# The output projection of a hybrid attention layer, summed in groups of two and four chunks in place of groups of two

## The chip, the cores and the metric

The kernel runs on one core of one Trainium2 chip. The metric is device time in microseconds (us) of one execution, lower is better; the kernel before stands at 1275.82 us, the median of three runs (1275.24 to 1278.71). Engines go by the names of the profile: PE is the matrix engine (PEld its weight loads), DVE the vector engine, ACT the scalar engine, POOL the general engine, SP the engine that issues the DMAs. A line such as L728 is line 728 of the kernel before.

## The reference, cut to what matters

One layer of width 1024 over 1024 tokens and 16 meta tokens. Three mixers read the same normalised input, their outputs are concatenated to 1024 columns and go through one projection, whose result is added to the residual; a gated feed-forward network follows.

```python
a = rmsnorm(h, norm1[i])
proj = a @ w_in[i]
...
y_pool = multiscale_pool_mixer(u, pool_w[i], pool_scale[i])
y_fox = head_rmsnorm(forgetting_attention(...), fox_out_gain[i], FOX_HEADS)
y_sb = head_rmsnorm(stick_breaking_attention(...), sb_out_gain[i], SB_HEADS)
h = h + jnp.concatenate([y_pool, y_fox, y_sb], axis=-1) @ w_out[i]
a = rmsnorm(h, norm2[i])
h = h + (jax.nn.silu(a @ w_gate[i]) * (a @ w_up[i])) @ w_down[i]
```

## The kernel before

Every fp32 product is made of three matmuls on split operands: each operand is split into a high part and the rest (tiles whose names end in h and l), and high times high, high times low and low times high are summed in PSUM.

The concatenated mixer output has eight chunks of 128 columns: 0 and 1 come from the pooling mixer, 2 to 4 from the forgetting heads, 5 to 7 from the stick-breaking heads. The six head pairs are worked one after another (`PAIRS`, L70), in the order of chunks 5, 2, 3, 4, 6, 7. Each finished chunk but the last is stored to HBM (`ysd`, L588); the last pair's result is kept on chip (`last_y`, L595).

The output projection (L690 to L763) takes the chunks in the groups `OGROUPS = ((5, 2), (3, 4), (0, 1), (6, 7))` (L782) and the tokens in two halves of 512 (j = 1, then j = 0). For a group and a half, `out_load` (L733) loads and splits what it needs: the group's weights once, by `split_weights` (L690), and the chunks' activations, by `split_y` (L711). Each 128x512 piece comes by a DMA on SP and is split by two instructions on POOL: a TENSOR_SCALAR for the high part (L77) and a TENSOR_TENSOR for the rest (L708 for weights, L717 for activations). `out_part` (L738) then calls `out_block` (L720) for each of four blocks of 128 tokens, and that for each 512 columns sums the group in one PSUM tile (six matmuls for two chunks, L728) and adds the tile into the residual `h` on DVE (L730). There are four groups, two halves, four blocks and two column halves, so 64 additions. The PSUM tiles have two buffers (tag `mm`). Of the split tiles there are few: group 0 and group 2 share four weight tiles `xa` of the pool `x0`, group 1 and group 3 share four tiles `wa`, and the split activations have eight tiles `xb`, two to a chunk, so eight tiles hold two parts of two chunks.

All this runs beside the attention of the last pairs. `interleave` (L815) takes steps of two streams in turn: `attention()` (L572) at a higher priority, and `filler()` (L857), which yields the projections of later pairs and then, from `open_out` (L840) on, the parts of the output projection in the order (0, 1), (0, 0), (1, 1), (1, 0), (2, 1), (2, 0) of group and half. The last group follows in `out_last` (L745), half 1 beside the attention's tail (L886), half 0 behind it (L933); for each block it also makes the norm of the finished rows on ACT (L753 to L760), and `turn_block` (L765) transposes them on PE (L771) for the feed-forward part. The framework then orders the instructions of each engine by its own forecast and the priorities, so the order on an engine is not that of the source. Each engine works its own list strictly in order.

The attention's own steps in these stretches: scores on PE (L465, L467, mask L470), ACT functions (L497 to L503), a scan on DVE (L506) and a subtraction (L508), an exponential (L510), transposes on PE (L560), their split by ACT (L563) and DVE (L564), and the weighted sum on PE (L549); at the end of a head pair's half a norm (L424 to L451, with a POOL split to `pt` and the matmuls L430, L431).

Behind it stands the feed-forward part: two column chunks are made directly (`direct`, L953), while DVE and ACT make sums and splits of the normalised rows (L974 to L981); then come ten rounds of a Strassen scheme (`strassen`, L992), whose products are matmuls of L917 on operands `t` and `s`, with weights that are combined on POOL (L1016, L999) and split by ACT (L903) and DVE (L905). The first combination needs a load of `w_gate` (L910) into space that the operands of those sums leave.

## Time and profile before

| what | value |
|---|---|
| median of three runs | 1275.82 us |
| the profiled execution's own time | 1275.61 us |
| its span, first to last instruction | 1273.8 us |
| outside the span | 1.8 us |
| mean granted PE clock | 0.986 |
| PE busy | 1214.1 us, 95% of the span |
| DVE busy | 904.7 us, 71% |
| ACT busy | 625.1 us, 49% |
| POOL busy | 469.2 us, 37% |

Output projection work on PE begins at 461.6 us of the span and ends at 626 us; the first Strassen product that needs a combined weight starts at 671.7 us. The page gives busy time, instructions and waits of each engine; "idle before" and what stands in square brackets is how long the engine waited for the instruction and which instruction released it. Matmuls overlap, so the pace of a stream of them is read from one start to the next and not from the duration of one.

### The profile page before, as it was taken

The numbers are of one execution on the slowest core, as the hardware profiler recorded it, in microseconds if no ns is written. First come the engines' busy times: TensorE is split into PE (matmuls) and PEld (weight loads), VectorE is DVE, ScalarE is ACT, GpSimd is POOL, SyncE is SP. The second block draws the span as 40 slices with busy tenths as digits, with TensorE's granted clock in tenths as the row PEclk, the third lists the DMA queues.
The fourth block names the chain that finished last, engine by engine and source line by source line (L and its number), as shares of the span: only waits on it lengthen the run. The fifth ranks groups of instructions, "written<-read, shape, count | busy, mean of one in ns | idle before, by whom it ended". The sixth has DMA issues, their size and how long they took to land.

```text
span 1273.8 us, 18454 instructions
## 1 busy us (share of the span) xinstructions
PE 1214.1 (95%) x6370; PEld 1027.3 (81%) x6370; DVE 904.7 (71%) x1573; ACT 625.1 (49%) x1283; POOL 469.2 (37%) x537
## 2 busy tenths in 40 slices
PE   7898899999898989998999999999999999999997
PEld 6787788899887877787787888888888888788885
DVE  6768866667857679997687667666676656866557
ACT  6567655455547676778644233333233334444443
POOL 3376154553366774440105444434444401000001
PEclk9899899999999989999999999999999999999999
DMA  8001010010110161101514545434555449576653
GB/s 327 30 17 35 10 59 19 30 38 26 42 34 25 47 240 51 58 25 67 191 57 142 190 165 159 155 127 156 190 172 167 134 137 334 173 223 195 194 174 140
DMA packets 74330, 151.38 MB, mean 119 GB/s; under 512 B 9197, under 2 KB 21485, under 8 KB 74237
## 3 DMA queue, kind: packets, MB, share of 16 engines
q1 hardware_dynamic: 70912, 146.27, 34.5%
q10 hardware_dynamic: 3324, 3.95, 0.9%
q8 instruction: 50, 0.82, 0.3%
q14 instruction: 44, 0.35, 0.1%
HBM read 108.24 MB, written 41.94 MB: 118 GB/s over the span
## 4 chain that ended last, share of the span: by engine, by line
PE 70%; DVE 14%; issue 6%; ACT 4%; DMA 4%; POOL 1%; SPq 0%; DVEq 0%; POOLq 0%; ACTq 0%
PE s L917 22%; PE mm L299 12%; PE mm L917 8%; PE s L1102 7%; PE mm L728 4%; DVE r L506 4%; PE o L549 4%; PE s L560 3%; PE mm L1102 3%; PE o L1102 3%; PE s L465 2%; PE s L467 1%; DVE P L508 1%; DMA wr<-in_w_in 1%; DVE pl L564 1%
## 5 line engine op out<-in xcount | busy, mean ns | idle before, releaser
L917 PE MATMUL s<-t,wh 128*128 128x512 f32 x544 | 170.2, 392 | 2.5 <-ACT wh L903 2.5
L917 PEld LDWEIGHTS s<-t,wh 128*128 128x128 f32 x544 | 102.8, 189 | 24.4 <-ACT wh L903 3.1
L917 PE MATMUL s<-s,wh 128*128 128x512 f32 x384 | 119.4, 391 | 0.3 <-ACT wh L903 0.3
L564 DVE TENSOR_TENSOR pl<-s,ph 128x512 fp32r<-128x512 f32 (+1 forms) x168 | 91.8, 568 | 32.4 <-ACT ph L563 28.5
L903 ACT CAST wh<-ss 128x512 fp32r<-128x512 f32 x80 | 49.5, 621 | 132.1 <-PE s L917 98.4
L563 ACT CAST ph<-s 128x512 fp32r<-128x512 f32 (+1 forms) x168 | 78.8, 493 | 67.0 <-PE o L549 38.3
L917 PE MATMUL s<-t,wl 128*128 128x512 f32 x272 | 106.1, 391 | 0.0
L917 PE MATMUL mm<-t,wh 128*128 128x512 f32 x320 | 98.7, 389 | 0.0
L1090 ACT CAST wh<-sg 128x512 fp32r<-128x512 f32 x74 | 46.0, 623 | 106.9 <-PE o L1102 45.2
L299 PE MATMUL mm<-x,wh 128*128 128x512 f32 (+1 forms) x320 | 97.8, 379 | 0.4 <-DVE pt L364 0.4
L903 ACT CAST wh<-raw 128x512 fp32r<-128x512 f32 x68 | 41.7, 620 | 108.4 <-PE s L917 69.9
L1091 DVE TENSOR_TENSOR wl<-sg,wh 128x512 fp32r<-128x512 f32 x74 | 50.9, 689 | 58.4 <-ACT wh L1090 58.1
L560 PE MATMUL s<-identr,P 128*128 128x128 f32 x528 | 82.6, 280 | 9.3 <-DVE P L508 4.1
L917 PEld LDWEIGHTS s<-s,wh 128*128 128x128 f32 x384 | 71.7, 188 | 15.8 <-ACT wh L903 1.1
L1011 DVE TENSOR_TENSOR cg<-s,tmp 128x512 f32<-128x512 f32 x60 | 41.3, 688 | 59.5 <-PE s L917 59.5
L549 PE MATMUL o<-pl,v 128*128 128x256 f32 (+1 forms) x288 | 82.5, 310 | 0.6 <-DVE pl L564 0.6
L299 PE MATMUL mm<-xa,wh 128*128 128x264 f32 (+3 forms) x248 | 77.5, 314 | 4.2 <-DVE v L358 3.8
L1141 POOL TENSOR_TENSOR r<-r,mhalf 128x1 f32<-128x1 f32 x8 | 4.4, 548 | 208.4 <-DVE r L1140 206.9
L560 PEld LDWEIGHTS s<-identr,P 128*128 128x128 f32 x528 | 63.6, 143 | 18.7 <-DVE pl L564 3.4
L549 PE MATMUL o<-ph,v 128*128 128x256 f32 (+1 forms) x288 | 77.6, 284 | 0.0
L299 PE MATMUL mm<-xb,wh 128*128 128x264 f32 (+3 forms) x248 | 76.9, 311 | 0.0
L299 PE MATMUL mm<-xa,wl 128*128 128x264 f32 (+3 forms) x248 | 76.5, 312 | 0.0
(290 smaller groups left out, 3548.2 us busy)
## 6 DMA issues: line engine op xcount, KB each, us to landing
sg<-lsd SPq DMA_DIRECT2D x70, 256.0 KB, 2.9
raw<-in_w_gate SPq DMA_DIRECT2D x22, 512.0 KB, 5.3
raw<-in_w_up SPq DMA_DIRECT2D x22, 512.0 KB, 4.0
wr<-in_w_in SPq DMA_DIRECT2D x80, 128.0 KB, 2.3
raw<-in_w_down SPq DMA_DIRECT2D x20, 512.0 KB, 3.5
lsd<-cg SPq DMA_DIRECT2D x40, 256.0 KB, 3.4
raw<-rsd SPq DMA_DIRECT2D x40, 256.0 KB, 3.4
raw<-in_w_down SPq DMA_DIRECT2D x34, 256.0 KB, 3.0
```

Of the source, the lines that this page charges most:

```text
L299: PE.matmul(p[:, :n], w[k][ww], xx(k, t0, n), start=i == 0, stop=i == 23)
L506: V.tensor_tensor_scan(r[:, ::-1], e[:, ::-1], (e if on_dve else r)[:, ::-1], 0.0 if prev is None else prev[:, 0:1], ALU.add, ALU.max if o ...
L549: PE.matmul(po[:, c:256], pr.v[h][:, kb, :], x, start=first and ix == 0, stop=(kb == nkb - 1 and ix == 1), skip_group_check=True)
L560: PE.transpose(tp[:, 128 * i:128 * i + 128], ptiles[ii][:, k0:k0 + 128], ident)
L563: S.copy(ph[:, :n], tp[:, :n])
L564: V.tensor_tensor(pl[:, :n], tp[:, :n], ph[:, :n], ALU.subtract)
L728: PE.matmul(p, y_[:, ts_], w_[:, ds], start=i == 0, stop=i == 3 * len(ws) - 1)
L903: S.copy(wh, a)
L917: PE.matmul(p, ws[ww][:, k, :], xs_[xx][:, k, :], start=first and i == 0, stop=i == 11, skip_group_check=True)
L1090: S.copy(wh, a)
L1091: V.tensor_tensor(wl, a, wh, ALU.subtract)
L1102: PE.matmul(p, x[xx][:, 128 * b:128 * b + 128], y[yy], start=first and i == 0, stop=last and i == 2, skip_group_check=True)
```

## The change

Groups can now be summed together: `out_load` and `out_part` take a tuple of groups. The order becomes group 0 for half 1, groups 0 and 1 together for half 0, groups 1 and 2 together for half 1, group 2 for half 0, and the last group for both halves as before. A joint part sums twelve matmuls in one PSUM tile and makes one addition for it, so 64 additions become 48. The matmuls, the loads and the splits are the same in number; a joint part holds all eight `xb` tiles at once. The lines below `out_load` move by up to three (L771 becomes L773, L917 becomes L920).

```diff
-    def out_load(g, j):
-        if g not in wts:
-            wts[g] = [split_weights(g, c) for c in OGROUPS[g]]
-        return [last_y[j] if c == PAIRS[5][3] else split_y(c, j) for c in OGROUPS[g]]
+    def out_load(gs, j):
+        for g in gs:
+            if g not in wts:
+                wts[g] = [split_weights(g, c) for c in OGROUPS[g]]
+        return [last_y[j] if c == PAIRS[5][3] else split_y(c, j) for g in gs for c in OGROUPS[g]]
...
-    def out_part(g, j, yy=None):
+    def out_part(gs, j, yy=None):
         if yy is None:
-            yy = out_load(g, j)
+            yy = out_load(gs, j)
         for tb in range(4):
-            yield from out_block(4 * j + tb, tb, yy, wts[g])
+            yield from out_block(4 * j + tb, tb, yy, [w for g in gs for w in wts[g]])
...
-        for g, j in ((0, 0), (1, 1), (1, 0), (2, 1), (2, 0)):
-            yield from out_part(g, j)
+        yield from out_part((0, 1), 0)
+        yield from out_part((1, 2), 1)
+        yield from out_part((2,), 0)
```

The first place is POOL's list where group 2's weights are split for the first time (`xa` from `wor`), with the activations of the next part (`xb` from `yr`); `pt` belongs to the attention's norm. Before, the weights (`xa`, `wor`) take turns with the activations of another part, group 1's half 0 (`xb_6995` to `xb_7003`):

```order
L77 TENSOR_SCALAR xa_7219<-wor_7221 128x512
L77 TENSOR_SCALAR xb_6995<-yr_6993 128x512
L77 TENSOR_SCALAR xa_7219<-wor_7225 128x512
L708 TENSOR_TENSOR xa_7220<-wor_7221,xa_7219 128x512
L717 TENSOR_TENSOR xb_6997<-yr_6993,xb_6995 128x512
L77 TENSOR_SCALAR xb_7001<-yr_6999 128x512
L708 TENSOR_TENSOR xa_7220<-wor_7225,xa_7219 128x512
L717 TENSOR_TENSOR xb_7003<-yr_6999,xb_7001 128x512
L77 TENSOR_SCALAR xa_7229<-wor_7231 128x512
```

In the changed kernel the same place on POOL, from the norm's split `pt` to the first part of chunk 0's activations (`xb_7011`), whose rest `xb_7013` comes three rows later and whose partner chunk 1 is split by the two rows after that:

```order
L717 TENSOR_TENSOR xb_7001<-yr_6997,xb_6999 128x512
L77 TENSOR_SCALAR xb_7005<-yr_7003 128x512
L77 TENSOR_SCALAR pt_6793<-nt_6791 128x512
L77 TENSOR_SCALAR xa_6987<-wor_6989 128x512
L717 TENSOR_TENSOR xb_7007<-yr_7003,xb_7005 128x512
L77 TENSOR_SCALAR xa_6987<-wor_6993 128x512
L77 TENSOR_SCALAR xb_7011<-yr_7009 128x512
L708 TENSOR_TENSOR xa_6988<-wor_6989,xa_6987 128x512
L708 TENSOR_TENSOR xa_6988<-wor_6993,xa_6987 128x512
L717 TENSOR_TENSOR xb_7013<-yr_7009,xb_7011 128x512
```

Eight weight splits, eight activation splits and one split of the norm now stand in one run behind one wait for PE, all of them ahead of the last matmuls of the first joint tile of groups 1 and 2; before, the weights of group 2 were split while group 1's own part had its operands already.

The second place is PE's list at the transposes of the last normalised block (L771 on `xa`), among the matmuls of the direct products; `s_8272` is the third of those products, `s_8299` the fourth. Before:

```order
L917 MATMUL s_8272<-s_7948,wl_8042 128x512
L771 MATMUL o_8180<-identr,xa_8136 128x128 x4
L917 MATMUL s_8299<-s_7945,wh_8046 128x512
L917 MATMUL s_8299<-s_7946,wh_8046 128x512
L917 MATMUL s_8299<-s_7945,wl_8048 128x512
L917 MATMUL s_8299<-s_7945,wh_8046 128x512
L771 MATMUL o_8186<-identr,xa_8136 128x128 x4
L917 MATMUL s_8299<-s_7946,wh_8046 128x512
```

In the changed kernel the third product is `s_8240`:

```order
L920 MATMUL s_8240<-s_7913,wl_8006 128x512
L920 MATMUL s_8240<-s_7913,wh_8004 128x512
L773 MATMUL o_8148<-identr,xa_8104 128x128 x4
L773 MATMUL o_8154<-identr,xa_8104 128x128 x4
L920 MATMUL s_8240<-s_7914,wh_8004 128x512
L920 MATMUL s_8240<-s_7913,wl_8006 128x512
```

The last transposes now stand in the third direct product and not in the fourth: from them to the first matmul that needs a combined weight there are 148 matmuls of that line in the list, where there were 128.

## The prediction

> **What bounds the kernel now.** I read the busy times first, then the stretches around the output projection, then who PE waited for there, and last the rows of each wait. The busy times say that PE is the bound:

> ```profile
> PE 1214.1 (95%) x6370; PEld 1027.3 (81%) x6370; DVE 904.7 (71%) x1573; ACT 625.1 (49%) x1283; POOL 469.2 (37%) x537
> ```

> The matmuls stay the same in number, so the change can only win or lose idle time of PE. The table of stretches (length, then busy time of PE, PEld, DVE, ACT and POOL, the granted clock, DMA) says where that is:

> ```profile
> 481.23:502.43 21.20, 19.49 (x109) 16.05 (x107) 18.30 (x32) 15.27 (x37) 6.47 (x7) 1.00 0.08 26
> 502.43:522.40 19.97, 17.21 (x79) 13.27 (x80) 19.03 (x29) 12.25 (x26) 15.68 (x15) 1.00 0.31 97
> ...
> 553.00:575.00 22.00, 21.60 (x121) 17.78 (x120) 21.36 (x37) 15.10 (x36) 4.47 (x4) 1.00 0.00 1
> 575.00:601.00 26.00, 23.00 (x147) 19.82 (x147) 19.33 (x41) 22.48 (x54) 1.24 (x2) 1.00 0.15 61
> 601.00:616.00 15.00, 11.68 (x53) 7.95 (x52) 14.88 (x25) 12.91 (x25) 1.09 (x2) 1.00 0.51 176
> ...
> 668.00:677.00 9.00, 6.53 (x22) 4.80 (x21) 5.37 (x5) 4.53 (x8) 7.21 (x6) 0.81 0.21 75
> 677.00:1273.80 596.80, 587.13 (x2589) 485.63 (x2587) 400.11 (x561) 207.41 (x357) 164.02 (x113) 1.00 0.54 177
> ```

> PE is idle for 1.7 and 2.8 us in the two stretches from 481 to 522, where groups 0 and 1 are summed, for 3.0 and 3.3 us at the end of the attention, and for 2.5 us near 670. Behind 677 it is idle for 9.7 us of 597, and the order there is the same in both kernels, so that part only shifts. From 502 to 522 DVE is busy for 19.03 of 19.97 us: there DVE is the rival of PE. The waits of PE, from 461 to 680 us (total, times, longest):

> ```profile
> PE mm L728 <- DVE x L730: 5.5, 7, 1.6
> ...
> PE s L917 <- ACT wh L903: 2.7, 2, 2.5
> PE s L560 <- DVE P L508: 2.2, 2, 1.8
> PE s L771 <- ACT xa L760: 1.7, 1, 1.7
> ```

> **Term A, the additions that go.** One addition takes 681 ns (minimum, median, maximum in the row), and 16 of them, 10.9 us of DVE, go:

> ```profile
> L730 DVE TENSOR_TENSOR x<-mm,x x64: 657/681/692, 465.2 to 626.2; 128x512 f32<-128x512 f32 x64
> ```

> DVE's time is not PE's. What PE feels is that a PSUM tile comes free late, when an addition stands behind the attention's scans. Four of the seven waits lie where tiles are now joined (the number in brackets is the wait):

> ```profile
> 502.43 1.66 PE L728 MATMUL mm<-wa,xb 128*128 128x512 f32 x6 [1.48 <-DVE x L730]
> ...
> 504.95 1.66 PE L728 MATMUL mm<-wa,xb 128*128 128x512 f32 x6 [0.20 <-DVE x L730]
> ...
> 507.70 1.67 PE L728 MATMUL mm<-wa,xb 128*128 128x512 f32 x6 [0.97 <-DVE x L730]
> ...
> 522.40 1.67 PE L728 MATMUL mm<-wa,xb 128*128 128x512 f32 x6 [1.57 <-DVE x L730]
> ```

> They sum to 4.2 us. A joint tile gives the addition twice the time, twelve matmuls and not six, 2.8 us and not 1.4 by the starts in the next rows; the longest wait, 1.57, is about what is added. I take A = -4.2; the bounds are 0 (other DVE work takes the place) and -5.5 (all seven).

> **Term B, the loads that can't run ahead.** The pace of PE's work, from starts: 12 matmuls in 2.82 us, 0.235 each; score matmuls 0.16 to 0.2; transposes 0.11, weighted sums 0.12:

> ```profile
> 513.97 0.32 PE L465 MATMUL s<-k,q 128*128 128x348 f32 x1
> 514.12 0.32 PE L467 MATMUL s<-k,q 128*128 128x348 f32 x1
> 514.28 2.97 PE L728 MATMUL mm<-wa,xb 128*128 128x512 f32 x12
> 517.10 0.32 PE L465 MATMUL s<-k,q 128*128 128x348 f32 x1
> ```

> ```profile
> 538.28 0.88 PE s L560 x8
> ...
> 542.48 0.48 PE o L549 x4
> ```

> And of POOL's splits (the last row of a run is its end; the brackets are waits):

> ```profile
> 480.19 0.62 POOL L77 TENSOR_SCALAR xb<-yr 128x512 fp32r<-128x512 f32 x1 [2.37 <-PE mm L728]
> 480.90 1.28 POOL L717 TENSOR_TENSOR xb<-yr,xb 128x512 fp32r<-128x512 f32 x1
> ...
> 499.80 1.28 POOL L77 TENSOR_SCALAR xa<-wor 128x512 fp32r<-128x512 f32 x1 [6.40 <-PE mm L728]
> ...
> 512.50 1.30 POOL L708 TENSOR_TENSOR xa<-wor,xa 128x512 fp32r<-128x512 f32 x1
> ...
> 537.43 0.63 POOL L77 TENSOR_SCALAR wa<-wor 128x512 fp32r<-128x512 f32 x1 [13.87 <-PE mm L728]
> ...
> 541.20 2.03 POOL L717 TENSOR_TENSOR xb<-yr,xb 128x512 fp32r<-128x512 f32 x1
> ...
> 545.04 1.31 POOL L717 TENSOR_TENSOR xb<-yr,xb 128x512 fp32r<-128x512 f32 x1
> ```

> At 499.80 POOL begins with group 2's weights as soon as group 0's last tile has read its own; the run of 12 splits ends at 513.80, 1.17 us each. PE did not wait for it, since group 1's part had its operands. In the changed kernel nothing lies between: the joint part of groups 1 and 2 needs all eight `xb` tiles, and the joint part ahead of it holds them to its last tile. Counted in the order, from the third matmul of that last tile (which frees the first `xa`) PE has 25 matmuls of the projection, 8 of scores, 2 of the norm, 17 transposes and 11 weighted sums ahead of the first matmul on the rest of chunk 0: 25 x 0.235 + 8 x 0.17 + 2 x 0.235 + 17 x 0.11 + 11 x 0.12 = 10.9 us. By then POOL has to make 15 splits (7 of the rest, 8 of the high part). At 0.62 and 1.28 they take 13.9 us, at 1.17 each 17.6. So PE halts for 3.0 to 6.7 us. The halt is in pieces, as each operand comes, and all that stands behind these matmuls in PE's list, the attention's transposes too, halts with it. DVE is less loaded here than at 499.80 but not idle, so I take 1.09 each, 16.4, and a halt of 5.5, nearer to the measured run of 12 than to the free pace. The DMAs of these pieces are issued ahead, except the last three, which wait for a buffer of POOL's and land within the run; SP has nothing else queued there.

> The next part, group 2 alone, has the same: the same eight splits as at 537.43, where chunk 0 was ready 5.8 us behind the release (541.20 + 2.03) and chunk 1 8.9 us (545.04 + 1.31). By the same paces PE has 5.0 and 8.1 us of work until it needs them, so 0.8 us more. At the first boundary there is none: chunk 3 and 4 of half 0 wait for PE as at 480.19, and their four splits are ready 4.4 us later, when PE is still in the first two chunks. B = +6.3, bounds 3.0 and 7.5.

> [...]

> **Term C, the end.** PE's list has the third direct product's matmuls behind the last transposes, 148 matmuls to the Strassen product with the first combined weight, where there were 128. In the profile:

> ```profile
> 639.53 0.60 PE L771 MATMUL o<-identr,xa 128*128 128x128 f32 x4
> ...
> 668.79 0.39 PE L917 MATMUL mm<-t,wl 128*128 128x512 f32 x1
> 671.66 1.74 PE L917 MATMUL s<-t,wh 128*128 128x512 f32 x4 [2.47 <-ACT wh L903]
> ...
> 675.88 0.39 PE L917 MATMUL s<-t,wh 128*128 128x512 f32 x1
> ```

> The chain from those transposes over DVE's sums, the load of `w_gate` (whose space they free), POOL and ACT takes 671.66 - 639.53 = 32.1 us. 128 matmuls take 29.1 (639.88 to 669.0, 0.228 each), 148 take 33.7; so PE would arrive 1.9 us behind the weight and not 2.5 ahead of it. The wait also costs pace: the 11 matmuls from 671.66 to 675.88 take 4.2 us for 2.5, since the clock was halved:

> ```profile
> 673.00:675.00 2.00, 2.00 (x6) 1.52 (x6) 2.00 (x3) 0.88 (x2) 1.52 (x1) 0.50 0.00 0
> ```

> ```profile
> 580.84 0.83 PE L560 MATMUL s<-identr,P 128*128 128x128 f32 x5 [1.84 <-DVE P L508]
> ```

> C = -(2.5 + 1.7) = -4.2, bounds 0 and -4.2. Next in line are the following weights, which stand ready behind 672 while PE takes 2.8 us for each product. A wait of 1.84 (above, 1.00 in its stretch) did not halve the clock and one of 2.47 did. Of B's pieces none is over 2.3 by the count; one over 2.5 would cost 1.7 more. [...]

> **Term D, the tail.** In 575 to 616 PE waits for the attention's last latency and for the norm of the blocks. The order puts two half tiles of the last group behind the attention's last weighted sums, where before they filled them: 6 matmuls, 1.4 us, if nothing else covers, 0 if they fill a later wait. D = +0.7. The rest of the 6.3 us idle there I leave as it is.

> **Sum.** The profiled execution took 1275.61 us, a span of 1273.8 and 1.8 around it, 0.2 below the median of the three. 1275.6 - 4.2 + 6.3 - 4.2 + 0.7 = 1274.2.

> **Rivals.** First, faster: POOL's run goes at its free pace, since DVE halts with PE and leaves it alone; B = 3.0 and D = 0, 1275.6 - 4.2 + 3.0 - 4.2 = 1270.2, and 1269 with all of A's bound. For it: splits of 0.62 and 1.28 stand in the rows; against: runs of a dozen never kept that pace.

> Second, slower: the halt is paid twice. In DVE's list the additions of the first two joint tiles of groups 1 and 2 stand ahead of the attention's next subtraction and scan, so DVE halts for POOL's run too, and its backlog moves into the stretch that was 553 to 575, where DVE was busy for 21.36 of 22.00 us; PE then waits there for the tiles as it did at 502, and A is 0. With B at 7.5, D at 1.4 and C as above: 1275.6 + 7.5 + 1.4 - 4.2 = 1280.3. It decides from a POOL run over 17.6 us (1.17 a split). Against it: DVE has 10.9 us less to do.

> Third, the change at the far end does not come: the chain to the first combined weight moves along with PE, and the 2.5 us and the slow clock stay: 1275.6 - 4.2 + 6.3 + 0.7 = 1278.4.

> **How the numbers follow.** A measurement of this kernel can tell about 0.3%, 3.8 us, from no change: faster is below 1272.0, slower above 1279.6. The forecast has 0.45 (its own range 1272 to 1277 by B's bounds), the first rival 0.30, the second 0.13, the third 0.12. Faster is most of the first rival and the forecast's lower end, 0.34; slower is the second and the third's upper end, 0.15; the rest, 0.51, is no change. The range goes from the first rival with A's bound, 1269, to the second, 1280.5.

> **What would show it.** Right: 48 additions, no wait of L728 for L730 over 0.5 us in the joint parts; waits of L728 for POOL's splits of 4 to 7 us in total, at the start of the joint part of groups 1 and 2; no wait of the first combined product, full clock there. The forecast is wrong if PE does not wait for POOL (then it is nearer 1270), or if waits for DVE's additions or scans come back behind that part, or if the wait near 670 is still there.

## The result, and the profile after

The changed kernel took 1282.21 us (median of 7 runs, 1280.84 to 1284.34), the kernel before 1278.08 beside it: a ratio of 1.0039, interval 1.0027 to 1.0051. A second set gave 1281.44 to 1277.76, 1.0022 (1.0010 to 1.0034). So the change makes the kernel slower by 0.2 to 0.4%, about 4 us. Both intervals lie above 1. The forecast was 1274.2, range 1269.0 to 1280.5, 1.4 us faster than its profiled execution: the sign was wrong, and the time lies above the range.

The profiled execution has a span of 1282.6 us, 8.8 longer than before, and not all of that is the change's: it is the slowest of its seven executions (1284.34 us), and that of the second profile the slowest of its eight (1283.94), while the forecast's profile of before (1275.61) lies near the fast end of the seven executions of before (1275.24 to 1278.71). The first page shows it: PE has the same 6370 matmuls, is busy for 6.9 us more and idle for 1.9 more, at a mean granted clock of 0.978 in place of 0.986.

```profile
PE 1221.0 (95%) x6370; PEld 1033.4 (81%) x6370; DVE 899.4 (70%) x1557; ACT 625.0 (49%) x1283; POOL 470.4 (37%) x537
```

Since both run 6370 matmuls, the start of the n-th can be laid beside the start of the n-th before. The difference grows or shrinks only where one of them loses time (us, against the first profile of before; "again" are second profiles of the same kernels):

| stretch of matmuls (times before) | before again | changed | changed again | forecast |
|---|---|---|---|---|
| 0 to 2340 (7 to 391), same list | +1.6 | +1.3 | +0.9 | |
| to 2470 (413), same list | +2.2 | +2.4 | +2.4 | |
| to 2860 (485), same list | +0.5 | -1.2 | -1.4 | |
| to 2990 (512) | 0.0 | -2.7 | -2.7 | A |
| to 3120 (539) | 0.0 | +7.6 | +7.7 | A's last wait, B |
| to 3640 (640) | +1.2 | +2.8 | +2.9 | B's second part, D |
| to 3870 (697) | -1.6 | -4.4 | -4.4 | C |
| to 5590 (1087), same list | 0.0 | 0.0 | 0.0 | |
| to 5720 (1118), same list | +0.9 | +3.0 | +3.0 | |

In the four rows where the lists differ, the changed kernel loses 3.2 and 3.4 us, where the forecast had a gain of 1.4. The rows above them are the same instructions in both kernels, and differ by as much between two profiles of one kernel. The waits of PE there, of the changed kernel from 511 to 535 us (engine and matmul, what it waited for, total, times, longest):

```profile
PE s L560 <- DVE P L508: 3.0, 2, 1.9
PE s L465 <- DVE P L508: 0.7, 1, 0.7
PE s L560 <- DVE pl L564: 0.7, 1, 0.7
PE mm L728 <- POOL xb L717: 0.6, 1, 0.6
PE o L431 <- DVE nt L428: 0.3, 1, 0.3
```

They add up to 5.3 us, nearly the 5.5 of the forecast halt, but 0.6 of it is for POOL's late pieces and 4.7 for DVE, whose part the forecast had at nothing. The table of stretches (length, busy PE, PEld, DVE, ACT, POOL, granted clock) says what more was lost:

```profile
505.00:513.10 8.10, 8.10 (x40) 6.56 (x39) 8.00 (x15) 3.90 (x9) 0.00 (x0) 1.00 0.09 34
513.10:526.60 13.50, 9.93 (x46) 6.71 (x45) 9.97 (x13) 10.35 (x23) 13.47 (x13) 1.00 0.25 78
526.60:536.80 10.20, 8.45 (x32) 6.95 (x31) 7.52 (x10) 5.35 (x11) 6.02 (x5) 0.50 0.41 129
536.80:561.00 24.20, 24.20 (x137) 20.57 (x137) 17.78 (x29) 14.43 (x34) 0.00 (x0) 1.00 0.00 1
561.00:580.00 19.00, 15.66 (x80) 12.09 (x79) 17.07 (x26) 13.07 (x33) 18.28 (x16) 1.00 0.14 43
```

From 505 to 513.1 PE is never idle: the waits of 502 to 508 us are gone, as forecast. Then POOL works its 17 splits without a break (POOL busy 13.47 of 13.50), PE idles for 3.6 us, and the clock stands at half for 10.2 us. A second run of POOL, 16 splits from 561, costs PE 3.3 us more, all of it waits for the additions, which stand behind the scans in DVE's list:

```profile
566.29 1.22 PE L728 MATMUL mm<-xa,xb 128*128 128x512 f32 x4 [0.43 <-DVE x L730]
...
571.89 3.05 PE L728 MATMUL mm<-xa,xb 128*128 128x512 f32 x12 [1.28 <-DVE x L730]
...
578.90 1.65 PE L728 MATMUL mm<-xa,xb 128*128 128x512 f32 x6 [1.61 <-DVE x L730]
```

Between the runs, with POOL idle, PE loses nothing.

What POOL's run does to DVE is seen in the groups of DVE's instructions by shape (busy time, mean ns of one), both in the changed kernel. From 497 to 513 us, where POOL is idle:

```profile
L508 DVE TENSOR_TENSOR P<-s,r 128x456 f32<-128x456 f32 x2 | 1.2, 614 | 0.0
...
L506 DVE TENSOR_TENSOR_SCAN r<-e 128x456 f32<-128x456 f32 x1 | 1.1, 1108 | 0.0
...
L506 DVE TENSOR_TENSOR_SCAN r<-e,r 128x348 f32<-128x348 f32 x1 | 0.9, 942 | 0.0
...
L451 DVE SCALAR_TENSOR_TENSOR nt<-op,gn,nt 128x512 f32<-128x512 f32 x1 | 0.7, 741 | 0.0
```

From 513 to 533 us, beside POOL's run:

```profile
L506 DVE TENSOR_TENSOR_SCAN r<-e,r 128x456 f32<-128x456 f32 x2 | 3.8, 1910 | 2.3 <-ACT e L503 2.3
...
L451 DVE SCALAR_TENSOR_TENSOR nt<-op,gn,nt 128x512 f32<-128x512 f32 x1 | 1.7, 1690 | 0.0
L506 DVE TENSOR_TENSOR_SCAN r<-e,r 128x348 f32<-128x348 f32 x1 | 1.5, 1540 | 0.0
...
L506 DVE TENSOR_TENSOR_SCAN r<-e,r,r 128x348 f32<-128x348 f32 x1 | 1.5, 1517 | 0.0
L508 DVE TENSOR_TENSOR P<-s,r 128x456 f32<-128x456 f32 x2 | 1.2, 617 | 0.0
L428 DVE TENSOR_TENSOR nt<-nt,pt 128x512 fp32r<-128x512 f32 x1 | 1.1, 1089 | 0.5 <-POOL pt L77 0.5
```

These scans (L506), the norm's product (L451) and L428 (0.69 alone), which read their operands from SBUF, take 1.6 to 2.3 times as long (one scan of 344 columns, at 524.18 us, takes 0.86 and 0.85 alone); the subtraction L508, which reads one operand from PSUM, takes 0.62 and 0.61. In the run DVE loses 4.1 us so, and POOL itself needs 19.6 us for splits that take 15.8 at 0.62 and 1.28. The same happens in the kernel before: over the same stretch of matmuls, 2860 to 3120, DVE loses about 2.5 us beside runs of 12 and 4 splits. So both take longer side by side than alone, DVE's scan of 456 columns 1.91 us for 1.11 and POOL's 17 splits 19.6 for 15.8; by what one holds up the other is not shown.

Single rows show how the longest of PE's waits comes about:

```profile
520.66 1.09 DVE L428 TENSOR_TENSOR nt<-nt,pt 128x512 fp32r<-128x512 f32 x1 [0.54 <-POOL pt L77]
...
521.17 1.71 POOL L717 TENSOR_TENSOR xb<-yr,xb 128x512 fp32r<-128x512 f32 x1
521.68 2.17 DVE L506 TENSOR_TENSOR_SCAN r<-e,r 128x456 f32<-128x456 f32 x1
...
525.62 0.66 PE L560 MATMUL s<-identr,P 128*128 128x128 f32 x4 [1.95 <-DVE P L508]
```

DVE waits 0.54 us for the norm's split `pt`, which stands among the others in POOL's run. Then L428 takes 0.4 us more than alone, and the scan, which begins while POOL's split L717 is under way, 1.0 to 1.1 more. These three make up the 1.95 us that PE waits. So a part of the waits for DVE is, one step back, a late piece of POOL's that DVE needed.

The last transposes do come early enough: the first product with a combined weight waits for nothing, at full clock.

```profile
678.90 0.39 PE L920 MATMUL mm<-t,wl 128*128 128x512 f32 x1
679.13 1.07 PE L920 MATMUL s<-t,wh 128*128 128x512 f32 x4
680.04 0.39 PE L920 MATMUL s<-t,wl 128*128 128x512 f32 x1
```

### The profile page after: what moved, and what is told of

It is laid out like the page before. It is cut to its first block, busy times and chain, and to the rows that moved or that the text cites. A ratio compares the mean times of both kernels' runs of the same rounds, so it can differ in the third digit from the quotient of the medians.

```text
span 1282.6 us, 18445 instructions
## 1 busy us (share of the span) xinstructions
PE 1221.0 (95%) x6370; PEld 1033.4 (81%) x6370; DVE 899.4 (70%) x1557; ACT 625.0 (49%) x1283; POOL 470.4 (37%) x537
## 4 chain that ended last, share of the span: by engine, by line
PE 79%; DVE 12%; ACT 4%; issue 2%; DMA 2%; POOL 1%; SPq 0%; DVEq 0%; POOLq 0%; ACTq 0%
PE s L920 25%; PE mm L299 13%; PE s L1105 9%; PE mm L920 8%; PE mm L728 5%; PE o L549 4%; PE s L560 3%; PE mm L1105 3%; PE o L1105 3%; DVE r L506 3%; PE s L465 2%; PE s L467 1%; DMA xk<-in_xtok 1%; DVE pl L564 1%; DVE P L508 1%
## 5 line engine op out<-in xcount | busy, mean ns | idle before, releaser
L920 PE MATMUL s<-t,wh 128*128 128x512 f32 x544 | 168.7, 389 | 0.0
L920 PEld LDWEIGHTS s<-t,wh 128*128 128x128 f32 x544 | 102.1, 188 | 21.2
L920 PE MATMUL s<-s,wh 128*128 128x512 f32 x384 | 118.9, 390 | 0.0
L564 DVE TENSOR_TENSOR pl<-s,ph 128x512 fp32r<-128x512 f32 (+1 forms) x168 | 91.8, 569 | 38.2 <-ACT ph L563 33.8
L920 PE MATMUL s<-t,wl 128*128 128x512 f32 x272 | 105.6, 389 | 0.0
L920 PE MATMUL mm<-t,wh 128*128 128x512 f32 x320 | 98.6, 389 | 0.0
L560 PE MATMUL s<-identr,P 128*128 128x128 f32 x528 | 84.2, 283 | 12.8 <-DVE P L508 6.2
L920 PEld LDWEIGHTS s<-s,wh 128*128 128x128 f32 x384 | 72.0, 188 | 14.9
L549 PE MATMUL o<-pl,v 128*128 128x256 f32 (+1 forms) x288 | 82.8, 311 | 0.6 <-DVE pl L564 0.6
L560 PEld LDWEIGHTS s<-identr,P 128*128 128x128 f32 x528 | 64.1, 145 | 22.7 <-DVE P L508 8.1
L549 PE MATMUL o<-ph,v 128*128 128x256 f32 (+1 forms) x288 | 78.5, 288 | 0.0
```

Source lines behind the costliest of these rows:

```text
L549: PE.matmul(po[:, c:256], pr.v[h][:, kb, :], x, start=first and ix == 0, stop=(kb == nkb - 1 and ix == 1), skip_group_check=True)
L560: PE.transpose(tp[:, 128 * i:128 * i + 128], ptiles[ii][:, k0:k0 + 128], ident)
L564: V.tensor_tensor(pl[:, :n], tp[:, :n], ph[:, :n], ALU.subtract)
L920: PE.matmul(p, ws[ww][:, k, :], xs_[xx][:, k, :], start=first and i == 0, stop=i == 11, skip_group_check=True)
```

## The experiments

Three theories stood at the start. Theory 1: POOL's run of splits, now in one piece, slows DVE's scans, PE waits for DVE, and its clock falls. Theory 2, the forecast's: PE waits for late pieces of POOL's. Theory 3: the difference is only where waits fall on the clock's steps. Times are medians; in brackets the ratio to the kernel before and its interval. (Some expectations put DVE's lengthening at 5.5 us; the sum over its instructions is 4.1.) A stretch is named by the matmul at which it ends, as in the table; the first boundary is the stretch to 3120, the second that to 3640.

**Both kernels again.** No edit.

> The kernel before once more, unchanged, for a second profile. Theory 1 (the changed stretch costs about 3 us, the rest of the difference between the two profiles is where waits fall on the clock's steps): 1278.4; half clock at other places than in the first profile, near 400 us or near 1085 us for one, and those alone make up what this profile differs from the first, up to 4 us; from 480 to 700 us it runs as the first did within 2 us. Theory 3 (all of the difference is that chance): this profile differs from the first by as much in 480 to 700 us as the changed kernel does, 3 us or more.

> The changed kernel once more, for a second profile: 1282. Theory 1: POOL's run of 17 splits at 510 to 533 us again, the same waits of PE for DVE's differences (L508) within 0.5 us, and 1 to 3 steps of half clock behind them; the stretch from 480 to 700 us costs 2 to 5 us more than before. Theory 3: under 1 us more.

The kernel before again: 1279.57 (1.0011, 0.9999 to 1.0022). The changed kernel again: 1281.44 (1.0022, 1.0010 to 1.0034). The stretch from 485 to 697 us differs by 0.4 us between the two profiles of before, and by 3.4 from the first of before in the changed kernel's second profile (3.2 in its first). The waits of the changed kernel come back to 0.2 us. Theory 3 falls for that stretch; it holds for what lies ahead of it. The same twelve instructions near 400 us, in the table of stretches of the first profile of before and of the changed kernel's:

```profile
399.00:402.40 3.40, 1.94 (x12) 1.58 (x12) 3.37 (x8) 3.35 (x11) 1.07 (x1) 1.00 0.34 113
402.40:405.80 3.40, 2.40 (x19) 2.15 (x18) 3.20 (x8) 3.35 (x11) 0.73 (x2) 1.00 0.00 0
```

```profile
400.30:403.70 3.40, 1.88 (x12) 1.57 (x12) 3.37 (x8) 3.35 (x11) 1.13 (x1) 1.00 0.33 115
403.70:410.50 6.80, 6.11 (x27) 5.64 (x26) 3.61 (x8) 6.75 (x17) 0.73 (x2) 0.50 0.00 0
```

**Only the additions gone.** The kernel before without 16 additions, loads and parts as they were:

```diff
...
-            V.tensor_tensor(h[b][:, ds], p, h[b][:, ds], ALU.add)
+            if not skip:
+                V.tensor_tensor(h[b][:, ds], p, h[b][:, ds], ALU.add)
...
+            yield from out_block(4 * j + tb, tb, yy, wts[g], (g, j) in ((0, 0), (1, 1)))
```

> The kernel before, with the 16 additions of group 0 half 0 and group 2's predecessor group 1 half 1 left out (their sums never reach the residual); loads, matmuls and parts as before; the last transposes fall at 1816 matmuls, which by itself gives the 4.2 of the far end. If the additions are what PE waits for (term A as forecast, -4.2): 1278.1 - 8.4 = about 1270. If POOL's run slows DVE's scans and the additions only stand behind them (theory 1): the scans of 500 to 514 us are as long as before, waits for L508 or L564 take the place of part of the waits for L730, A is -2 or less: 1272 to 1274. Theory 3: 1276 to 1282.

1269.66 (0.9929, 0.9917 to 0.9940). To matmul 3120 it gains 3.9 us, at the far end 4.4. So terms A and C, together 8.4, were sized rightly, and theory 1's guess of a smaller A missed: DVE was slowed here too (3.4 us in all, beside POOL's runs of 12 and 5), but without the additions DVE had room for it, and PE waited 1.2 us.

**One joint part alone.** In the first kernel groups 1 and 2 are apart, in the second groups 0 and 1:

```diff
-        yield from out_part((1, 2), 1)
+        yield from out_part((1,), 1)
+        yield from out_part((2,), 1)
```

```diff
-        yield from out_part((0, 1), 0)
+        yield from out_part((0,), 0)
+        yield from out_part((1,), 0)
```

> Groups 0 and 1 joined for half 0 alone; groups 1 and 2 of half 1 apart again; 56 additions, and 1815 matmuls of the Strassen line behind the last transposes as in the changed kernel (1816), not 1796 as before. Theory 1 (POOL's run of splits in front of the joint part of groups 1 and 2 shuts DVE's scans out, PE waits for their differences and its clock halves): the run lies beside group 1's part again, so the loss is gone and only the gain at the far end is left, 1278.1 - 4.2 = about 1274, with no half clock between 500 and 545 us. Theory 2 (PE waits for late pieces of POOL's): the same time, since the pieces are early again. Theory 3 (the two kernels differ by where halts fall on the clock's grid, nothing else): 1276 to 1282 with half clock at any place.

> Groups 1 and 2 joined for half 1 alone; group 0 and group 1 of half 0 apart; 56 additions, 1815 matmuls behind the last transposes. Theories 1 and 2: the joint part that needs all eight activation tiles is there, so the loss of 7 to 10 us is there, less 4.2 at the far end: 1281 to 1284. Theory 1 expects PE's waits there to be for L508's differences and L564, 3 us or more, and under 1 us for POOL; theory 2 over 3 us for POOL. Theory 3: 1276 to 1282 without a common place.

1274.12 (0.9962, 0.9950 to 0.9974) and 1278.65 (1.0000, 0.9989 to 1.0010). The first time is as theory 1 expected, but not by the expected way, for its loss and its half clock did not go: POOL's run behind groups 0 and 1 is still 17 splits long (510.7 to 530.2 us), PE waits 4.6 us for DVE, and only one step of half clock follows where the changed kernel has three; the stretch to 3120 loses 4.7, not 7.6, and the next gains 1.7. The second time was missed by theories 1 and 2 (1281 to 1284) and lies in theory 3's range: POOL's first run is 12 splits, in its old place, with most of the old waits for L730 (3.5 us); the kernel loses 1.0 and 2.4 at the two boundaries and gains the 4.4. So it is the part of groups 0 and 1 that makes the first run long, and in both kernels PE waits for DVE behind the joint part's loads (4.6 us, and 5.9 from 545 to 590 us).

**Copies in place of subtractions.** The changed kernel with each of group 2's rests as two copies of one operand (printed for the weights; the activations' lines are alike):

```diff
-                G.tensor_tensor(wl[:, qs], raw, wh[:, qs], ALU.subtract)
+                if g == 2:
+                    hi_pool(wl[:, qs], raw)
+                    hi_pool(wl[:, qs], raw)
+                else:
+                    G.tensor_tensor(wl[:, qs], raw, wh[:, qs], ALU.subtract)
...
```

> The changed kernel, in which the rest of each split of group 2 (weights and activations) is made by two one-operand copies (L77's form, 0.62 us each) in place of one subtraction of two SBUF operands (1.28): POOL's run is as long, but only one operand is read at a time; the low parts are then wrong, which leaves the three-term product of group 2 wrong. The last transposes fall at 1798 matmuls, so the 4.2 of the far end are lost. Theory 1 (two-operand splits shut out DVE's scans): scans in the run at their free time (456 wide 1.16, not 1.65 to 2.17), PE's waits for L508 there under 1 us, no half clock: 1282.2 - 8 + 4.2 = about 1278. Theory 2 (the pieces are late): the run takes as long, the loss stays: 1282.2 + 4.2 = about 1286.

1279.49 (1.0003, 0.9992 to 1.0014), near theory 1's 1278 and far from theory 2's 1286, but not for the reason given. The scans beside the copies were slowed too:

```profile
L506 DVE TENSOR_TENSOR_SCAN r<-e,r 128x456 f32<-128x456 f32 x2 | 3.5, 1744 | 2.3 <-ACT e L503 2.3
```

PE's waits from 511 to 535 came to 3.7 us in smaller pieces, spread over DVE and POOL, and no step of half clock followed: the stretch lost 2.7 where the changed kernel lost 7.6. In all DVE lost 2.4 us in place of 4.1. So copies of one operand on POOL slowed these scans too, though less (1.74 us, where it was 1.91 beside the subtractions and 1.11 alone), and the larger part of what the edit saved is the clock: PE's idle time no longer lay in one step.

**POOL's work by itself.** The kernel before with idle work on POOL, first in small pieces (48 additions of 128 columns), then nine of 512 columns behind its last split:

```diff
...
+            for n in range(48):
+                qs = slice(128 * (n % 4), 128 * (n % 4) + 128)
+                G.tensor_tensor(scr, yy[1][0][:, qs], yy[1][1][:, qs], ALU.add)
```

```diff
...
     y6 = split_y(OGROUPS[g][0], 0)
+    for _ in range(9):
+        G.tensor_tensor(lastraw[0], y6[0], y6[1], ALU.add)
...
```

> The kernel before with 48 additions of 128 columns on POOL (operands on SBUF, into a tile that nobody reads), 34 of them behind its last split, where POOL was idle from 560 to 580 us; each other engine's list is as before, instruction by instruction, and nobody waits for these additions. Theory 1 (work on POOL by itself slows DVE's scans, and PE waits for DVE): scans of 400 and 264 columns there take 1.1 to 2 us in place of 0.99 and 0.70, DVE, busy for 97% of that stretch, falls back by 3 to 5 us, PE waits for it by 2 to 5 us: 1280 to 1284. Theory 2 (only late pieces of POOL's hold PE up): 1278.4, no change.

> The kernel before with nine more additions of 512 columns on POOL (both operands on SBUF, into a tile that nobody reads any more), all behind its last split, where POOL was idle from 560 to 580 us; every other engine's list is as before, instruction by instruction. Theory 1 (the splits slow DVE's two-operand instructions and so PE): the scans of 264 and 400 columns there grow from 0.70 and 0.99 to 1.2 to 2, DVE's list by 2 to 4 us in all, PE waits for L730 and L508 by 2 to 4 us more between 560 and 590; nothing is late on POOL, since the nine end before 579. About 1281. Theory 2 (only late pieces hold PE up): 1278, waits as in the kernel before.

The small pieces: 1282.72 (1.0037, 1.0025 to 1.0049), in theory 1's range and yet no proof of it. They took 0.64 us each, not the 0.4 that their number was planned by, ran until 586.2 us, and held back the norm's split; PE waited 2.4 us for that. The scans were slowed by about 1 us in all.

The nine large ones: 1280.08 (1.0020, 1.0009 to 1.0030). They end at 574.4, POOL is then idle for 9.7 us, and nothing is late. Every list but POOL's is that of the kernel before. The scans beside them, and those of the second profile of before at the same work:

```profile
L506 DVE TENSOR_TENSOR_SCAN r<-e,r 128x264 f32<-128x264 f32 x2 | 3.0, 1488 | 0.0
L506 DVE TENSOR_TENSOR_SCAN r<-e 128x400 f32<-128x400 f32 x1 | 1.9, 1898 | 0.0
L506 DVE TENSOR_TENSOR_SCAN r<-e 128x264 f32<-128x264 f32 x1 | 1.1, 1118 | 0.0
```

```profile
L506 DVE TENSOR_TENSOR_SCAN r<-e,r 128x264 f32<-128x264 f32 x2 | 1.5, 728 | 0.0
L506 DVE TENSOR_TENSOR_SCAN r<-e 128x400 f32<-128x400 f32 x1 | 1.0, 991 | 0.0
L506 DVE TENSOR_TENSOR_SCAN r<-e 128x264 f32<-128x264 f32 x1 | 0.7, 695 | 0.0
```

DVE loses 2.9 us, and PE's waits there go from 0.3 us (first view, the second profile of before) to 2.4 (second view; the addition has moved to L733 in this kernel):

```profile
PE mm L728 <- DVE x L730: 0.3, 1, 0.3
```

```profile
PE mm L731 <- DVE x L733: 2.4, 2, 1.4
```

So POOL's work alone, for which nobody waits, costs PE time through DVE. That is theory 1's first link, shown by itself.

**A shorter run.** The changed kernel with group 2's rests never made (first edit, printed for the weights); with the weights' high parts on ACT (second edit, its first two lines); with all high parts of groups 1 to 3 on ACT (second edit, whole); and the kernel before with the whole second edit:

```diff
-                G.tensor_tensor(wl[:, qs], raw, wh[:, qs], ALU.subtract)
-        return wh, wl
+                if g != 2:
+                    G.tensor_tensor(wl[:, qs], raw, wh[:, qs], ALU.subtract)
+        return wh, wh if g == 2 else wl
...
```

```diff
-                hi_pool(wh[:, qs], raw)
+                S.copy(wh[:, qs], raw)
...
-        hi_pool(yh, raw)
+        (hi_pool if regions["wo"] is None else S.copy)(yh, raw)
```

> The changed kernel with the rests of group 2's weights and activations never made (the high parts are read in their place, which leaves that part of the sum wrong); POOL's run shrinks from 17 splits to about 9, 8 of them copies; the matmuls are the same in number. The last transposes fall at 1798 matmuls, so 4.4 of the far end are lost. Theory 1: DVE's lengthening in the run 2.5 us or less, PE's waits between 510 and 535 under 2 us and no half clock there; the end of group 2's part as in the changed kernel (+2): 1277 to 1279. Theory 3 or another cause of the waits (the joint tiles themselves): waits of 4 us or more stay, 1283 to 1286.

> The changed kernel with the high parts of the weights of groups 1 to 3 made on ACT, 12 copies of 0.62 us, four of them out of POOL's run of 17; 1815 matmuls behind the last transposes, so the far end keeps its gain. Theory 1: DVE's lengthening in the run falls from 5.5 us to about 4, PE's waits there from 5.3 to 3 to 4, fewer steps of half clock: 1277 to 1280. Theory 2 (pieces late): the run ends 2.5 us earlier, PE waits for POOL 0: the same 1278. If ACT's exponentials are held up: 1282 or more.

> The changed kernel with all 28 high parts of groups 1 to 3 on ACT: POOL's run of 17 becomes 9, subtractions of two operands but for one. 1798 matmuls behind the last transposes: the far end's 4.4 are lost. Theory 1: DVE's lengthening about 4 us at the first run and under 2 at the second (group 3), PE's waits there 3 and 2: 1280 to 1282. Theory 2: no piece late, 1279. If ACT's exponentials are held up: 1284 or more.

> The kernel before with the high parts of the splits of groups 1 to 3 made by ACT in place of POOL (28 copies of 0.62 us move); 1815 matmuls behind the last transposes, so the far end gains its 4.2. Theory 1: POOL's runs are shorter by a third, fewer scans meet them, PE's waits for L730 at 500 to 525 us shrink from 4.2 to 2 or less: 1271 to 1273. Theory 2 (only lateness counts; no piece was late before): 1274. If ACT's exponentials come late by the moved copies: 1276 or more.

Without the rests: 1279.93 (1.0016, 1.0007 to 1.0024). PE waits for nothing at all from 505 to 535 us: the joint tiles cost nothing, and to matmul 3120 this kernel gains 3.2. More than that is lost at the second boundary (5.7, the changed kernel 2.8), which no theory had: PE waits 5.1 us for L508 there, all behind 572 us, when POOL's run of 12 has been over since 557.5, and two steps of half clock follow. So POOL's run is not the whole cause at the second boundary.

The weights' high parts on ACT: 1275.69 (0.9982, 0.9973 to 0.9991), about 6 us faster than the changed kernel. DVE's lengthening in the run, now of 13 splits, falls from 4.1 to 2.0 us, PE waits 3.2, and no half clock follows there (the second boundary still costs 3.7):

```profile
PE mm L728 <- POOL xa L708: 1.2, 1, 1.2
PE mm L728 <- POOL xb L77: 0.9, 2, 0.6
PE s L560 <- DVE P L508: 0.8, 2, 0.5
PE mm L728 <- DVE x L730: 0.3, 1, 0.3
```

Two of three microseconds are now for POOL's late pieces: theory 2's wait exists, and is next in line once DVE is quicker.

All high parts on ACT (24 copies, not the 28 of the expectation): 1275.81 (0.9988, 0.9977 to 0.9998), although its last transposes stand late; it loses 1.5 and 1.2 at the two boundaries, and near 677 us there is no half clock, so the far end still gives 0.8. The forecasts of 1279 to 1282 were too high: ACT had the room (from 505 to 530 us PE waits 0.3 us for it). The same edit on the kernel before: 1272.51 (0.9953, 0.9941 to 0.9965), 1.4 us from the output projection, 4.4 from the far end. It is the fastest that computes the reference, and joins no groups.

## Why the prediction was wrong, step by step

Of the 8.0 us between the forecast (1274.2) and the measured time, 2.5 are its base: it started from one fast execution, 1275.6, where the kernel before measured 1278.1 beside the changed one. Another 4.6 lie in the four rows of the table where the lists differ, a gain of 1.4 forecast and a loss of 3.2 found. The rest, 0.9, is not traced.

**A, the additions that go, -4.2.** Right: the three waits of 502 to 508 us are gone (-2.7 to matmul 2990), and the kernel without additions gains 3.9.

**B, the loads that can't run ahead, +6.3.** This is the step that failed. The place, the length of POOL's run (19.6 us for 17; 17.6 for 15 had been the far end) and the sum of the waits (5.3 to 5.5) were as forecast. Two things were not. First, who is waited for: the step took PE to halt "in pieces, as each operand comes", on POOL, and gave DVE's part no cost: PE waited 0.6 us for POOL and 4.7 for DVE. That the two slow each other stood in the rows that the prediction quoted, but only from POOL's side (2.03 for a split of 1.28, 1.28 for one of 0.62). Second, the clock: "Of B's pieces none is over 2.3 by the count; one over 2.5 would cost 1.7 more". The longest piece was 1.95 us, and yet the clock was at half for three steps:

```profile
523.20:526.60 3.40, 1.45 (x9) 0.92 (x9) 3.40 (x6) 2.36 (x5) 3.40 (x3) 1.00 0.22 77
526.60:530.00 3.40, 2.34 (x9) 1.64 (x8) 3.40 (x4) 1.71 (x4) 3.40 (x3) 0.50 0.38 110
530.00:533.40 3.40, 2.71 (x14) 2.42 (x13) 3.14 (x5) 1.90 (x4) 2.62 (x3) 0.50 0.62 199
533.40:536.80 3.40, 3.40 (x13) 2.90 (x12) 0.98 (x2) 1.75 (x5) 0.00 (x0) 0.50 0.24 77
```

Behind a step with 1.45 us of work the clock is at half, in the next two steps PE is still idle for 1.75 us in all, and the clock comes back behind a step without idle time. (In the kernel with nine additions it came back behind one with 2.7 us of work at half clock, near 584 us.) To matmul 3120, A and B were to come to +1.3 (the 5.5 of the first boundary less 4.2); they came to 4.9. The 3.6 between are about what the half clock cost: in its 10.2 us PE was busy for 8.45, at a granted clock of 0.50, an estimated 4.2 us lost. Both profiles of the changed kernel have these three steps; whether its faster executions have them too is not shown. Over all its executions the granted clock is 0.978 to 0.983, that of the kernel before beside the second set 0.981 to 0.986.

Of the prediction's own signs of being wrong, the waits for scans and additions came. The other, that PE does not wait for POOL, nearly came, but the time near 1270 that it was to bring did not.

**The second boundary and D, +0.8 and +0.7.** 2.8 and 2.9 were measured. To matmul 3440 (596 us before) the loss was 4.7, and the tail behind it gained 1.9, where D had it lose 0.7. The wait was again not the one named: beside the run of 16 splits for group 3 the scans are slowed (one of 400 columns took 2.01 us, 0.98 alone), and the additions stand behind them, with the 3.3 us of waits for L730. That the run is all of the cause is not shown: the kernel without the rests loses more there with a shorter run.

**C, the end, -4.2.** Right in place: all six kernels with 1815 or 1816 matmuls behind the last transposes gain 4.4 against the first profile of before. Its size hung on that profile: in the second profile of before the wait is 2.23 us and the clock stays full, so against it C is 2.8. Here the size was partly luck.

**Rivals.** The second rival had the right sign and the right carrier, DVE, and also the place and the wait of its second payment: the stretch that was 553 to 575 lies at 560 to 586 us in the changed kernel, and the 3.3 us of waits for L730 fall there. Its reason fails: no backlog moved there, since from 537 to 561 us DVE is busy for 17.8 of 24.2 us and PE is never idle; a second run of POOL stands beside these waits. Nor was A 0, and the half clock was in none of its terms. These errors went against each other, so that its 1280.3 is near the measured time is luck. The first rival's free pace did not come (19.6 us for 17 splits), nor did the third's loss of the far end.

**What stays open.** Whether more buffers (four more weight tiles, 16 KB a partition) would undo the loss was not tried. In the kernels with a shorter run of POOL the lists of PE and DVE differ from the changed kernel's too, from about 520 us on or earlier; only in the kernels with idle additions is every other list as it was, and there it is the kernel before. So how much of the first boundary's loss is the run and how much the order of the lists is not separated. The wait near 1090 us, in lists that are equal, is 1.13 us in the first profile of before, 2.00 in the second, 2.55 and 2.50 in the changed kernel's, and 1.2 to 3.0 in others; with one step of half clock it makes 3.0 us. That the change has a part in it (through the time at which loads start) was not tried. How much work in a step keeps the clock is not settled either: one step with 2.1 us of work, near 327 us in the first profile of before, was followed by half clock, and one with 1.48 us, near 674 us in the second, was not.

## What to carry to other kernels

A run of work on POOL was not free here just because nobody waited for it: nine additions cost DVE 2.9 us, and PE's waits for DVE went from 0.3 to 2.4 us. Look up what DVE's scans and its other instructions on SBUF operands take alone and beside such a run (a scan of 400 columns took 0.99 and 1.90 us), and whose wait ends on them. Joining tiles to save instructions joins their loads too, and the buffers that let loads run ahead are taken up by the joined part. In these runs a stall's cost in clock went by the work left to PE in a step of 3.4 us more than by its longest piece: a wait of 1.95 us in the changed kernel stood in a step with 1.45 us of work and had three steps of half clock behind it, one of 1.84 in the first profile of before fell on steps with 2.15 and 2.13 and had none. And of a difference of a few microseconds, first take off what stretches with equal lists show between two profiles of one kernel.

## What the runs showed of the hardware that was not expected

The same wait of 1.84 us (transposes of L560 for L508) left the clock at full in the first profile of before, where it fell across two steps with 2.15 and 2.13 us of work; in the second half clock followed, where the step had 1.82:

```profile
576.50:579.90 3.40, 2.15 (x18) 1.72 (x16) 1.92 (x5) 3.32 (x12) 0.00 (x0) 1.00 0.01 2
579.90:583.30 3.40, 2.13 (x13) 1.74 (x14) 3.37 (x9) 3.40 (x10) 0.62 (x1) 1.00 0.00 0
```

```profile
581.40:584.80 3.40, 1.82 (x15) 1.42 (x14) 2.22 (x5) 3.35 (x12) 0.00 (x0) 0.99 0.01 2
584.80:588.20 3.40, 2.81 (x12) 2.65 (x13) 3.33 (x9) 2.65 (x8) 0.62 (x1) 0.51 0.00 0
```

Additions of 128 columns on POOL took 0.64 us each in a row, half of what a split's subtraction of 512 takes alone (1.28), and slowed the scans far less: 1 us over 34 of them (21.6 us), against 2.9 over nine large ones (14.2 us).
